# One masked minimum per score block, and the past's stages tied to their place, in a decoder-trunk kernel

## The chip, the cores and the metric

The kernel runs on one core of one Trainium2 chip. The metric is the device time of one execution in microseconds. The core has a matrix engine (TensorE, PE in the profile), a vector engine (VectorE, DVE), an activation engine (ScalarE, ACT), a general engine (GpSimd, POOL) and an engine that here only issues transfers (SyncE, SP). Each works through its own list of instructions in order, and semaphores tie the lists to one another.

## The reference

One inference step of one layer, for a prompt of 512 tokens and eight sample tokens that share the weights. All is fp32.

```python
m = ada_modulation(c)                           # shift, scale, gate, twice
h = rms_norm(x) * (1 + sc1) + sh1
xr, gr, q, k, v, fl, ga, gb = split(h @ w_in)   # D = 1024, 16 heads of 64
xc = causal_dwconv(xr, conv_buf, conv_w, conv_b)          # width 4
A = (rg_lru(xc) * gelu(gr)) @ w_proj_a
logf = log_sigmoid(fl + b_f);  F = cumsum(logf)
s = q.k / 8 + F[t] - F[s'],  masked to s' <= t            # prompt: blocks of 128 queries
B = (softmax(s) @ v) @ w_proj_b
x = x + g1 * ((sigmoid(ga) * A + sigmoid(gb) * B) @ w_o)
x = x + g2 * SwiGLU(rms_norm(x) * (1 + sc2) + sh2)        # then a last norm
```

The eight sample tokens attend to a paged cache of 1024 keys and values each (eight pages of 128 rows for each token), joined with their own new key and value. Their convolution takes the three inputs before from a state.

## The kernel before

Weights and activations are split into a high and a low part, and each product is three matmuls for each k-tile of 128 rows (high by high, low weight, low activation; L245, `half_product`). The 520 tokens are the free dimension, in two halves of 260. One product is a column tile of 128; its weights arrive by DMA (`wraw`), ACT makes the high part (`whi`, L210) and DVE the low one (`wlo`, L211), several products ahead.

A scheduler orders the instructions of each engine by a cost that it simulates while the program is built. An edge that adds no wait, `tc.issue_after(ins)`, keeps what follows behind `ins` on that instruction's engine; it can only shape the order.

Stages, in us of the profiled execution: norm, modulation and query products to 95; then eight rounds of convolution, recurrence and gates to 300; the first key product, branch A's projection and the first scores to 365; eight turns of prompt attention to 585, which this document numbers 1 to 8; branch B's projection and the merge to 640; the output projection to 700; and the FFN to the end.

A turn handles two heads. PE's list in turn n: the half `k_0` of the next key product; transposes of the value tile (`vt`); the half `k_1`; transposes of the probabilities (`ptt`); the half `v_0`; the second head's `ptt`; the next heads' first score blocks (`sc`); `v_1`; the values of the prompt (`po`); the other score blocks. ACT casts the keys (`ksA`, `ksB`, L985, the low parts by DVE at L988), the values (L1030) and the transposed probabilities (`ph`, L1086), takes the exponentials (L1067) and scales half of the probabilities (L1073). The last turn runs the last gate products instead of a key and a value product.

The decay rows of the two next heads (`decay_rows`) come in on SP as a broadcast of 512 numbers (`fb`, L1039); POOL adds the causal mask for the diagonal blocks (`fm`, L1041). In `scores`, DVE's custom operation adds decay and score and keeps the minimum over the row (scores carry a negative sign): once over the columns left of the diagonal block (L1064) and once over the diagonal block (L1065), which starts from the first minimum. Each is followed by a read of the accumulator. The minimum is the bias of the exponential.

The past runs beside all that in small steps, issued by `tick` (L644) at each product and four times a turn (`KEYS_AT`, `VALUES_AT`). Each key page of 512 KB is multiplied by the query and reduced on DVE (L629, L630). For two sample tokens at a time, a chain of five stages (`past_softmax`) then gives the weights of the past. Its last stage (`lgs`, L688) writes the sums out to memory through ACT (`mtd<-row`), and the last of the four chains has them loaded back (`mb<-mtd`). Value pages are multiplied on PE by calls of four matmuls (`pv`, L710), 32 calls in all; after each eighth, DVE picks the diagonal (`dr`, L716, L718), and a fold (`pvs`, L725, PE; copied by ACT) is issued at the next call. `join_weights` in the last turn joins past and present; its first DVE operation on loaded data is `mp`, L1138. In the convolution, three small DVE operations (L831) add the state's terms for the sample columns, in each of eight rounds.

Of the kernel before, what the change touches and what calls it, by code (L numbers as in the profile page):

```python
# [1 line left out]

# [6 lines left out]
F32 = mybir.dt.float32  # L9
F32R = mybir.dt.float32r  # L10
I32 = mybir.dt.int32
AF = mybir.ActivationFunctionType
ALU = mybir.AluOpType
AX = mybir.AxisListType
# [4 lines left out]
NP = 512  # L19
NS = 8  # L20
# [4 lines left out]
KT = 8  # L25
# [3 lines left out]
HALF = NT // 2  # L29
# [35 lines left out]
def kernel(ctx, tc, xT, par, gates, b_f, cst, cse, own, cache_k, cache_v, cache_lf, pt,  # L65
# [13 lines left out]
    def slot(name, cols=NT, dt=F32, parts=128):  # L79
        return heap.tile([parts, cols], dt, name=name, tag="slot")  # L80
# [4 lines left out]
    def small(name, parts, cols, bufs=4):  # L85
        return sm.tile([parts, cols], F32, name=name, tag="s_" + name, bufs=bufs)
# [151 lines left out]
    def half_product(n, j, a, out):  # L238
        hi, lo = splits[n]
        nk = units[n][2]  # L240
        t0, t1 = HALVES[j]
        for k in range(nk):
            ah, al = a(k, j) if callable(a) else (v[:, t0:t1] for v in a[k])
            for m, (wt, at) in enumerate(((hi, ah), (lo, ah), (hi, al))):
                pe.matmul(out[:, :HALF], lhsT=wt[k], rhs=at, start=k == 0 and m == 0, stop=k == nk - 1 and m == 2)  # L245

    def run_later(n):
        for fn in later.pop(n, []):
            fn()

    def product(name, a, evac, mid=None):
        n = begin()
# [390 lines left out]

    def tick(keys, values):  # L644
        key_sums()
        for c in list(chains):
            c[0] += 1
            if c[0] >= 2:
                c[0] = 0
                if next(c[1], True):  # L650
                    chains.remove(c)
        state["due"] += values
        state["due"] -= some_values(min(1, state["due"]))
        value_pages()
        key_pages(keys)

# [46 lines left out]
    def sample_values(r, j):  # L703
        if j == 0:
            pv[0] = bank(f"pv{r}")
        pgs = ahead.pop(0)
        for gq in range(4):
            c = 32 * j + 8 * gq
            hf = gq % 2
            pe.matmul(pv[0][32 * gq:32 * gq + 32, :], lhsT=pw[r][:, c:c + 32],  # L710
                      rhs=pgs[gq // 2][:, 512 * hf:512 * hf + 512], start=j == 0, stop=j == NPAGE - 1,
                      tile_position=(0, 32 * gq))
        if j == NPAGE - 1:
            pw[r] = None
            dr = slot("dr", 512)
            dve.tensor_tensor(dr, pv[0], pvm, ALU.mult)  # L716
            for n in (256, 128):
                dve.tensor_tensor(dr[:, :n], dr[:, :n], dr[:, n:2 * n], ALU.add)  # L718
            pv["todo"] = r, dr
        elif "todo" in pv:  # L720
            fold_values(*pv.pop("todo"))

    def fold_values(r, dr):
# [13 lines left out]
    def some_values(n):  # L737
        done = 0
        while done < n and values_todo and pw[values_todo[0][0]] is not None:
            value_pages()  # L740
            sample_values(*values_todo.pop(0))
            value_pages()
            done += 1
        return done
# [14 lines left out]
    def q_samples(b):  # L759
        t = slot("qt", 512, parts=NS)  # L760
        act.activation(t, qtp[b], AF.Copy, scale=DH ** -0.5)
        sp.dma_start(qtd[:, 512 * b:512 * b + 512], t)

    ready = []
    for i in range(KT):
        if i % 4 == 0:
            qtp.append(bank(f"qt{i}", NS))
        if i < 6:
            t = qpart[i]
            for j, (t0, t1) in enumerate(HALVES):  # L770
                b = bank(f"q{i}_{j}")
                for k in range(4):
                    q_matmuls(1, i, j, k, b)
                dve.tensor_tensor(t[:, t0:t1], b[:, :HALF], t[:, t0:t1], ALU.add)
        else:
            t = slot("q")
            product(f"q{i}", h, to(t, act.copy))
        if ready:
            q_done(*ready.pop())
        ready.append((i, t))  # L780
        if i == 3:
            split_upto(0)
        if i == 4:
            past_load()
            split_upto(1)
            close = forget_logits()
        if i == 6:
            close()
            with tc.issue_after(state["last"].ins), tc.issue_after(state["act"].ins):
                decay()  # L790
            past_turn(0)
        if i == 7:
            past_turn(1)
        if i >= 2:
            ada_piece(1, i - 2)
# [16 lines left out]
    def conv(i):  # L812
        gr = gate_load(i)
        if i + 1 < KT:
            gate_load(i + 1)
        xr, xc = slot("xr"), slot("xc")

        def evac(j, b):
            t0, t1 = HALVES[j]
            act.copy(xr[:, t0:t1], b)  # L820
            act.activation(xc[:, t0:t1], b, AF.Identity, scale=cw[3], bias=prm[:, i, P_CB:P_CB + 1])

        cw = [prm[:, i, P_CW + n:P_CW + n + 1] for n in range(4)]
        sc = prm[:, i, P_SC:P_SC + 24].rearrange("p (s n) -> p n s", n=3)
        co = conv_out[:, i, 3:27].rearrange("p (s n) -> p n s", n=3)
        product(f"xr{i}", h, evac)
        for n in range(3):
            d = 3 - n
            dve.scalar_tensor_tensor(xc[:, d:NP], xr[:, :NP - d], cw[n], xc[:, d:NP], ALU.mult, ALU.add)
        for n in range(3):  # L830
            dve.scalar_tensor_tensor(xc[:, NP:], sc[:, n], cw[n], xc[:, NP:], ALU.mult, ALU.add)  # L831
        pool.tensor_copy(conv_out[:, i, 0:3], xr[:, NP - 3:NP])
        pool.tensor_copy(co[:, 0:2], sc[:, 1:3])
        pool.tensor_copy(co[:, 2], xr[:, NP:])
        lru[i] = {"xc": xc}

        def close():
            gw = slot("gws", 512, F32R)
            act.copy(gw[:, :256], gr)
            dve.tensor_tensor(gw[:, 256:], gr, gw[:, :256].bitcast(F32), ALU.subtract)  # L840
            del gate_raw[i]
            lru[i].update(xs=split("xc", xc), gw=gw)

        defer(0, close)
# [188 lines left out]

    fbs, prob, pts = {}, {}, {}

    def decay_rows(i):
        for hd in (2 * i, 2 * i + 1):
            fb = slot("fb", 512)
            sp.dma_start(fb, ftd[hd:hd + 1, :].partition_broadcast(128))  # L1039
            fm = slot("fm", 512)  # L1040
            pool.tensor_tensor(fm.rearrange("p (b c) -> p b c", b=4), fb.rearrange("p (b c) -> p b c", b=4),  # L1041
                               msk.unsqueeze(1).to_broadcast([128, 4, 128]), ALU.add)
            fbs[hd] = fb, fm

    def scores(i, blocks):
        ks = kvs[i]["k"]
        qq, ql = kvs[i]["q"]
        mus = small("mu", 128, 16, 4).rearrange("p (c b a) -> p c b a", c=4, b=2)
        for b in blocks:
            n = 128 * b  # L1050
            for a, pr in enumerate(HEADS):
                hd = 2 * i + a
                fb, fm = fbs[hd]
                if b == 0:
                    prob[hd] = []
                    t3 = slot("p3", 512), slot("p02", 512), slot("p1", 256)
                    pts[hd] = (t3[1][:, :128], t3[2], t3[1][:, 128:], t3[0])
                sc = bank(f"sc{hd}_{b}")
                pe.matmul(sc[:, :n + 128], lhsT=qq[a][:, n:n + 128], rhs=ks[a][:, :n + 128], start=True, stop=False)
                pe.matmul(sc[:, :n + 128], lhsT=ql[a][:, n:n + 128], rhs=ks[a][:, :n + 128], start=False, stop=True)  # L1060
                p = pts[hd][b]
                mu = mus[:, :, b - blocks[0], a]
                if b:
                    dve.tensor_tensor_reduce(p[:, :n], fb[:, :n], sc[:, :n], 1.0, 3.0e38, ALU.add, ALU.min, mu[:, 0:1])  # L1064
                dve.tensor_tensor_reduce(p[:, n:n + 128], fm[:, n:n + 128], sc[:, n:n + 128], 1.0,  # L1065
                                         mu[:, 0:1] if b else 3.0e38, ALU.add, ALU.min, mu[:, 1:2])
                act.activation(p[:, :n + 128], p[:, :n + 128], AF.Exp, bias=mu[:, 1:2], scale=-1.0, accum_out=mu[:, 2:3])  # L1067
                prob[hd].append((p, mu))
        dve.reciprocal(mus[:, 3], mus[:, 2])
        for b in blocks:  # L1070
            for a in range(2):
                p, mu = prob[2 * i + a][b]
                (pool.tensor_scalar(p, p, mu[:, 3:4], None, ALU.mult) if a and i + 1 < KT else act.activation(p, p, AF.Copy, scale=mu[:, 3:4]))  # L1073

    def turn(i, a):
        hd = 2 * i + a
# [120 lines left out]
    for i in range(KT):  # L1197
        last = i + 1 == KT

        def mid_a():  # L1200
            v_tokens(i)
            if last:
                turn(i, 0)
            at(i, 0)
            if last:
                join_weights()

        def mid_b():
            if not last:
# [300 lines left out]
```

## Time and profile before

| | |
|---|---|
| median of three runs | 1085.54 us (1084.76 to 1086.71) |
| the profiled execution | 1088.77 us |
| its span, first to last instruction | 1087.0 us |
| mean granted TensorE clock | 0.981 |
| busy: PE, PEld, DVE, ACT, POOL | 96%, 88%, 62%, 46%, 14% |
| read from and written to HBM | 192.5 and 13.1 MB |

PE is matmul, PEld the load of weights beside it. An engine's row of 40 digits cuts the span into slices of 27.2 us, each digit the busy share in tenths. A wait is put down to the instruction whose end came last; "idle before" is time in which the engine had nothing that could start. In a row of matmuls the number before the colon of each form is partitions by columns. The turns start at about 367.8, 401.1, 426.9, 455.8, 482.2, 506.6, 543.2 and 565.8 us, where the first matmul of the key product (in the last turn, the gate) starts.

### The profile page before, as it was taken

The numbers are of one execution on the slowest core, as the hardware profiler recorded it, in microseconds if no ns is written. First come the engines' busy times: TensorE is split into PE (matmuls) and PEld (weight loads), VectorE is DVE, ScalarE is ACT, GpSimd is POOL, SyncE is SP. The second block draws the span as 40 slices with busy tenths as digits, with TensorE's granted clock in tenths as the row PEclk, the third lists the DMA queues.
The fourth block names the chain that finished last, engine by engine and source line by source line (L and its number), as shares of the span: only waits on it lengthen the run. The fifth ranks groups of instructions, "written<-read, shape, count | busy, mean of one in ns | idle before, by whom it ended". The sixth has DMA issues, their size and how long they took to land.

```text
span 1087.0 us, 20916 instructions
## 1 busy us (share of the span) xinstructions
PE 1038.3 (96%) x8210; PEld 954.5 (88%) x8210; DVE 674.6 (62%) x1261; ACT 495.1 (46%) x967; POOL 153.6 (14%) x201
## 2 busy tenths in 40 slices
PE   4999999999979989899799999999999999999996
PEld 2888999999969967687588989999999999999996
DVE  6434799979899988976375545943344333433355
ACT  4423576856831556677386224543212323222352
POOL 1102010100022514443130001500000000000013
PEclk9999999999989989999899999999999999999998
DMA  9796776689879998989843783222322422323212
GB/s 337 259 350 201 236 264 201 191 270 265 267 226 320 306 287 251 336 226 318 287 168 123 253 298 87 78 79 78 111 84 78 117 79 82 113 79 91 85 59 79
DMA packets 164996, 206.94 MB, mean 190 GB/s; under 512 B 9490, under 2 KB 125730, under 8 KB 164834
## 3 DMA queue, kind: packets, MB, share of 16 engines
q1 hardware_dynamic: 161170, 198.70, 58.5%
q10 hardware_dynamic: 3648, 6.39, 1.6%
q8 instruction: 64, 1.05, 0.4%
q0 software_dynamic: 80, 0.52, 0.2%
q14 instruction: 34, 0.28, 0.1%
HBM read 192.49 MB, written 13.09 MB: 189 GB/s over the span
## 4 chain that ended last, share of the span: by engine, by line
PE 76%; DVE 8%; DMA 6%; issue 4%; ACT 3%; POOL 1%; SPq 0%; POOLq 0%; DVEq 0%; ACTq 0%
PE fiu L245 11%; PE fig L245 11%; PE fo L245 8%; PE xr L245 4%; PE pb L245 4%; PE ga L245 4%; PE gr L245 3%; PE gb L245 3%; PE v L245 3%; PE k L245 3%; PE wo L245 3%; PE pa L245 2%; DMA pg<-in_cache_k_dram 2%; PE qp L450 2%; PE pv L710 2%
## 5 line engine op out<-in xcount | busy, mean ns | idle before, releaser
L211 DVE TENSOR_TENSOR wlo<-wraw,whi 128x1024 fp32r<-128x1024 f32 (+1 forms) x131 | 164.3, 1254 | 147.2 <-ACT whi L210 147.2
L210 ACT CAST whi<-wraw 128x1024 fp32r<-128x1024 f32 (+1 forms) x131 | 136.6, 1043 | 210.6 <-PE fo L245 74.7
L245 PE MATMUL fig<-h2h,whi 128*128 128x260 f32 x320 | 90.5, 283 | 0.0
L245 PE MATMUL fiu<-h2h,whi 128*128 128x260 f32 x320 | 90.5, 283 | 0.0
L245 PE MATMUL fiu<-h2h,wlo 128*128 128x260 f32 x320 | 90.5, 283 | 0.0
L245 PE MATMUL fig<-h2h,wlo 128*128 128x260 f32 x320 | 90.5, 283 | 0.0
L245 PE MATMUL fiu<-h2l,whi 128*128 128x260 f32 x320 | 90.2, 282 | 0.0
L245 PE MATMUL fig<-h2l,whi 128*128 128x260 f32 x320 | 90.2, 282 | 0.0
L245 PE MATMUL fo<-ach,wlo 128*128 128x260 f32 x292 | 82.7, 283 | 0.0
L245 PE MATMUL fo<-acl,whi 128*128 128x260 f32 x292 | 82.7, 283 | 0.0
L245 PE MATMUL fo<-ach,whi 128*128 128x260 f32 x292 | 82.5, 282 | 0.0
L630 DVE TENSOR_REDUCE S<-pg 128x16 f32<-128x1024 f32 x64 | 76.6, 1211 | 1.3 <-POOL pg L617 1.0
L629 DVE TENSOR_TENSOR pg<-pg,qb 128x1024 f32<-128x1024 f32 x60 | 74.8, 1260 | 3.0 <-DMA pg<-in_cache_k_dram 3.0
L320 POOL TENSOR_TENSOR ss<-ss,sq 128x260 f32<-128x260 f32 x18 | 13.6, 755 | 422.7 <-ACT sq L319 422.3
L245 PEld LDWEIGHTS fiu<-h2l,whi 128*128 128x128 f32 x320 | 60.3, 189 | 0.0
L245 PEld LDWEIGHTS fig<-h2l,whi 128*128 128x128 f32 x320 | 60.3, 189 | 0.0
L245 PEld LDWEIGHTS fig<-h2h,wlo 128*128 128x128 f32 x320 | 60.3, 188 | 0.0
L245 PEld LDWEIGHTS fiu<-h2h,wlo 128*128 128x128 f32 x320 | 60.3, 188 | 0.0
L245 PEld LDWEIGHTS fig<-h2h,whi 128*128 128x128 f32 x320 | 60.3, 188 | 0.0
L245 PEld LDWEIGHTS fiu<-h2h,whi 128*128 128x128 f32 x320 | 60.3, 188 | 0.0
L245 PEld LDWEIGHTS fo<-ach,whi 128*128 128x128 f32 x292 | 55.1, 189 | 0.0
L245 PEld LDWEIGHTS fo<-ach,wlo 128*128 128x128 f32 x292 | 55.0, 188 | 0.0
(378 smaller groups left out, 3380.2 us busy)
## 6 DMA issues: line engine op xcount, KB each, us to landing
pg<-in_cache_k_dram SPq DMA_DIRECT2D x64, 512.0 KB, 5.7
pg<-in_cache_v_dram SPq DMA_DIRECT2D x64, 512.0 KB, 6.2
araw<-in_ada_w_dram SPq DMA_DIRECT2D x48, 512.0 KB, 7.3
wraw<-in_w_fi_dram SPq DMA_DIRECT2D x44, 512.0 KB, 5.2
wraw<-in_w_in_dram SPq DMA_DIRECT2D x34, 512.0 KB, 8.2
wraw<-in_w_in_dram SPq DMA_DIRECT2D x11, 1024.0 KB, 6.3
wraw<-in_w_fo_dram SPq DMA_DIRECT2D x8, 1024.0 KB, 5.2
x<-in_xT_dram SPq DMA_DIRECT2D x16, 260.0 KB, 5.8
```

The lines of the kernel that those rows point to most:

```text
L210: state["act"] = act.copy(hi[:, :k1 - k0], src)
L211: state["last"] = dve.tensor_tensor(lo[:, :k1 - k0], src, hi[:, :k1 - k0].bitcast(F32), ALU.subtract)
L245: pe.matmul(out[:, :HALF], lhsT=wt[k], rhs=at, start=k == 0 and m == 0, stop=k == nk - 1 and m == 2)
L320: eng.tensor_tensor(acc[:, t0:t1], acc[:, t0:t1], q_, ALU.add)
L450: pe.matmul(b[:, :HALF], lhsT=wt, rhs=at[:, t0:t1], start=k == 0 and m == 0, stop=k == 3 and m == 2)
L629: dve.tensor_tensor(pg, pg, q, ALU.mult)
L630: dve.tensor_reduce(S[r // 2][:, c:c + H], pg.rearrange("p (h d) -> p h d", d=DH), AX.X, ALU.add)
L710: pe.matmul(pv[0][32 * gq:32 * gq + 32, :], lhsT=pw[r][:, c:c + 32], rhs=pgs[gq // 2][:, 512 * hf:512 * hf + 512], start=j == 0, stop=j == ...
```

## The change

Four edits.

The minimum of a block is taken by one DVE operation over all its columns. So decay and mask stand side by side in the block's own order: ACT copies the first 256 columns of `fb` into `fm`, POOL adds the mask to four pieces of 128 columns (one of them in `fb`, one into a new small tile `f0`). Block 0 reads `f0`, block 1 two pieces of `fm`, block 2 the first 384 columns of `fm`, and block 3 `fb`. A row of `mu` falls away.

The steps of the chains and of the past's values in `tick`, and `join_weights` in the last turn, are held behind the last product matmul on PE, the last weight split on DVE and the last on ACT that the program had written by then (`in_place`). Key pages are not.

The fold of a finished group is issued at the third call of the next group, not at its first.

The state's terms of the convolution are computed once for all eight rounds (`past_conv`, eight products and one sum in the query stage), and each round adds them with one DVE operation.

```diff
@@ half_product
             for m, (wt, at) in enumerate(((hi, ah), (lo, ah), (hi, al))):
-                pe.matmul(out[:, :HALF], lhsT=wt[k], rhs=at, start=k == 0 and m == 0, stop=k == nk - 1 and m == 2)
+                state["mm"] = pe.matmul(out[:, :HALF], lhsT=wt[k], rhs=at, start=k == 0 and m == 0,
+                                        stop=k == nk - 1 and m == 2)
...
+    @contextmanager
+    def in_place():
+
+        with tc.issue_after(state["mm"].ins), tc.issue_after(state["last"].ins), tc.issue_after(state["act"].ins):
+            yield
@@ tick
         key_sums()
-        for c in list(chains):
...
-        state["due"] += values
-        state["due"] -= some_values(min(1, state["due"]))
+        with in_place():
+            for c in list(chains):
...
+            state["due"] += values
+            state["due"] -= some_values(min(1, state["due"]))
         value_pages()
         key_pages(keys)
@@ sample_values
-        elif "todo" in pv:
+        elif j == 2 and "todo" in pv:
             fold_values(*pv.pop("todo"))
@@ the query stage
+    conv_past = keep.tile([128, KT, NS], F32, name="conv_past")
+
+    def past_conv():
+        t = slot("cvp", KT * 24).rearrange("p (k s n) -> p k s n", k=KT, s=NS)
+        for i in range(KT):
+            dve.tensor_tensor(t[:, i], prm[:, i, P_SC:P_SC + 24].rearrange("p (s n) -> p s n", n=3),
+                              prm[:, i, P_CW:P_CW + 3].unsqueeze(1).to_broadcast([128, NS, 3]), ALU.mult)
+        dve.tensor_reduce(conv_past, t, AX.X, ALU.add)
...
                 decay()
+                past_conv()
             past_turn(0)
@@ conv
-        for n in range(3):
-            dve.scalar_tensor_tensor(xc[:, NP:], sc[:, n], cw[n], xc[:, NP:], ALU.mult, ALU.add)
+        dve.tensor_tensor(xc[:, NP:], xc[:, NP:], conv_past[:, i], ALU.add)
@@ decay_rows
         for hd in (2 * i, 2 * i + 1):
+            a = hd % 2
+            if a == 0:
+                f0 = slot("f0", 256)
             fb = slot("fb", 512)
             sp.dma_start(fb, ftd[hd:hd + 1, :].partition_broadcast(128))
             fm = slot("fm", 512)
-            pool.tensor_tensor(fm.rearrange("p (b c) -> p b c", b=4), fb.rearrange("p (b c) -> p b c", b=4),
-                               msk.unsqueeze(1).to_broadcast([128, 4, 128]), ALU.add)
-            fbs[hd] = fb, fm
+            act.copy(fm[:, :256], fb[:, :256])
+            for dst, b in ((f0[:, 128 * a:128 * a + 128], 0), (fm[:, 384:], 1), (fm[:, 256:384], 2), (fb[:, 384:], 3)):
+                pool.tensor_tensor(dst, fb[:, 128 * b:128 * b + 128], msk, ALU.add)
+            fmb = fm.rearrange("p (b c) -> p b c", b=4)
+            fbs[hd] = f0[:, 128 * a:128 * a + 128], fmb[:, 0::3], fm[:, :384], fb
@@ scores
-                if b:
-                    dve.tensor_tensor_reduce(p[:, :n], fb[:, :n], sc[:, :n], 1.0, 3.0e38, ALU.add, ALU.min, mu[:, 0:1])
-                dve.tensor_tensor_reduce(p[:, n:n + 128], fm[:, n:n + 128], sc[:, n:n + 128], 1.0,
-                                         mu[:, 0:1] if b else 3.0e38, ALU.add, ALU.min, mu[:, 1:2])
...
+                ins = p[:, :n + 128], sc[:, :n + 128]
+                if b == 1:
+                    ins = [t.rearrange("p (b c) -> p b c", b=2) for t in ins]
+                dve.tensor_tensor_reduce(ins[0], fbs[hd][b], ins[1], 1.0, 3.0e38, ALU.add, ALU.min, mu[:, 0:1])
...
@@ the last turn
             if last:
-                join_weights()
+                with in_place():
+                    join_weights()
```

Three places show how the order moves. The first is PE's list in turn 6, from the last transposes of the first probabilities to the value product; a row of `pv` with x4 is one call. Before:

```order
L1082 MATMUL ptt_1_7310<-cs,p_7025 128x128
L1082 MATMUL ptt_1_7310<-cs,p_7024 128x128 x2
L688 MATMUL lgs_7319<-mk,cs 128x32
L710 MATMUL pv_7324<-pg,pw 32x512 x20
L725 MATMUL pvs_7329<-cs,dr 128x16
L245 MATMUL v_0_7366<-hh,whi 128x260
```

And now:

```order
L1105 MATMUL ptt_1_7332<-cs,p_7044 128x128
L1105 MATMUL ptt_1_7332<-cs,p_7043 128x128 x2
L696 MATMUL lgs_7341<-mk,cs 128x32
L718 MATMUL pv_7346<-pg,pw 32x512 x4
L245 MATMUL v_0_7385<-hh,whi 128x260
L245 MATMUL v_0_7385<-hh,wlo 128x260
```

Of the five calls that stood there one is left, and the fold is gone from this place. By the calls in PE's list, turns 1 to 8 held 3, 3, 3, 4, 3, 5, 2.25 and 0.75 calls, in 4, 5, 3, 6, 4, 5, 3 and 1 groups of up to four matmuls; now they hold 3, 3, 3, 3, 3, 3, 4 and 2, in 3, 3, 3, 4, 3, 3, 5 and 2. Most turns now have one call behind `vt`, one behind the first `ptt` and one at the turn's end. Eight calls stand ahead of turn 1, as before.

The second is DVE's list in turn 6, where the first operation of `join_weights` on the loaded sums stood between a weight split and the key splits. Before:

```order
L1008 SCALAR_TENSOR_TENSOR qlB<-qB,qqB 128x512
L211 TENSOR_TENSOR wlo<-wraw,whi 128x1024
L1138 TENSOR_TENSOR mp<-mb,lf 16x8
L988 TENSOR_TENSOR ksA<-k_0_7198,ksA 64x260
L988 TENSOR_TENSOR ksB<-k_0_7198,ksB 64x260
L1031 TENSOR_TENSOR v_7233<-vt_7228,v_7233 128x2x128
```

Now it stands a turn later, among the minima (ISA rows) of the last scores at the end of turn 7:

```order
L1089 ISA p_7827,mu<-fm,sc_1_7838 128x256
L1089 ISA mu 128x1
L1092 RECIPROCAL mu<-mu 128x4
L211 TENSOR_TENSOR wlo<-wraw,whi 128x1024
L1161 TENSOR_TENSOR mp<-mb,lf 16x8
L1089 ISA p_7818,mu<-fm,sc_2_7931 128x384
```

The third is ACT's list in turn 5, from the weight split to the key and value casts. Before:

```order
L210 CAST whi<-wraw 128x1024
L985 CAST ksA<-k_0_6810 64x260
L985 CAST ksB<-k_0_6810 64x260
L986 COPY kt<-k_0_6810 128x260
L1030 CAST v_6845<-vt_6840 128x2x2x64
```

And now:

```order
L210 CAST whi<-wraw 128x1024
L1063 COPY fm<-fb 128x256 x2
L1002 CAST ksA<-k_0_6829 64x260
L1002 CAST ksB<-k_0_6829 64x260
L1003 COPY kt<-k_0_6829 128x260
L1047 CAST v_6864<-vt_6859 128x2x2x64
```

The two copies of the decay rows, which wait for the rows to land, stand between the split and the casts. On SP a load of a value page (`pg<-in_cache_v`) stands ahead of the second row in turns 5, 6 and 7, and it waits until the `pv` call behind `vt` of the same turn has freed a page's place.

More of the change, by code (lines that the diff above doesn't have):

```diff
@@ L1 @@
-from contextlib import ExitStack, nullcontext
+from contextlib import ExitStack, contextmanager, nullcontext
 import numpy as np
@@ L645, in tick @@
         key_sums()
-        for c in list(chains):
[L647 to L651, printed above, removed]
-        state["due"] += values
-        state["due"] -= some_values(min(1, state["due"]))
+        with in_place():
+            for c in list(chains):
+                c[0] += 1
+                if c[0] >= 2:
+                    c[0] = 0
+                    if next(c[1], True):
+                        chains.remove(c)
+            state["due"] += values
+            state["due"] -= some_values(min(1, state["due"]))
         value_pages()
@@ L1047, in scores @@
         qq, ql = kvs[i]["q"]
-        mus = small("mu", 128, 16, 4).rearrange("p (c b a) -> p c b a", c=4, b=2)
+        mus = small("mu", 128, 12, 4).rearrange("p (c b a) -> p c b a", c=3, b=2)
         for b in blocks:
@@ L1052, in scores @@
                 hd = 2 * i + a
-                fb, fm = fbs[hd]
                 if b == 0:
@@ L1062, in scores @@
                 mu = mus[:, :, b - blocks[0], a]
-                if b:
-                    dve.tensor_tensor_reduce(p[:, :n], fb[:, :n], sc[:, :n], 1.0, 3.0e38, ALU.add, ALU.min, mu[:, 0:1])
-                dve.tensor_tensor_reduce(p[:, n:n + 128], fm[:, n:n + 128], sc[:, n:n + 128], 1.0,
-                                         mu[:, 0:1] if b else 3.0e38, ALU.add, ALU.min, mu[:, 1:2])
-                act.activation(p[:, :n + 128], p[:, :n + 128], AF.Exp, bias=mu[:, 1:2], scale=-1.0, accum_out=mu[:, 2:3])
+                ins = p[:, :n + 128], sc[:, :n + 128]
+                if b == 1:
+                    ins = [t.rearrange("p (b c) -> p b c", b=2) for t in ins]
+                dve.tensor_tensor_reduce(ins[0], fbs[hd][b], ins[1], 1.0, 3.0e38, ALU.add, ALU.min, mu[:, 0:1])
+                act.activation(p[:, :n + 128], p[:, :n + 128], AF.Exp, bias=mu[:, 0:1], scale=-1.0, accum_out=mu[:, 1:2])
                 prob[hd].append((p, mu))
-        dve.reciprocal(mus[:, 3], mus[:, 2])
+        dve.reciprocal(mus[:, 2], mus[:, 1])
         for b in blocks:
@@ L1072, in scores @@
                 p, mu = prob[2 * i + a][b]
-                (pool.tensor_scalar(p, p, mu[:, 3:4], None, ALU.mult) if a and i + 1 < KT else act.activation(p, p, AF.Copy, scale=mu[:, 3:4]))
+                (pool.tensor_scalar(p, p, mu[:, 2:3], None, ALU.mult) if a and i + 1 < KT else act.activation(p, p, AF.Copy, scale=mu[:, 2:3]))
     def turn(i, a):
```

## The prediction

> **What bounds the kernel now.** I read the page first: the first line is the busy time of each engine, the next three cut the span into 40 slices of 27.2 us (tenths).
>
> ```profile
> PE 1038.3 (96%) x8210; PEld 954.5 (88%) x8210; DVE 674.6 (62%) x1261; ACT 495.1 (46%) x967; POOL 153.6 (14%) x201
> PE   4999999999979989899799999999999999999996
> PEclk9999999999989989999899999999999999999998
> DMA  9796776689879998989843783222322422323212
> ```
>
> TensorE is the bound. Work taken from another engine is worth nothing unless PE stands still for it, so the question is where PE has holes that the change touches. Slices with a 7 stand at 11 and 19. The table of stretches shows the convolution's stage (95 to 300 us) and then, about turn by turn, the eight prompt-attention turns (us; PE, PEld, DVE, ACT, POOL busy; granted clock, DMA share, GB/s).
>
> ```profile
> 95.00:300.00 205.00, 205.00 (x1671) 193.78 (x1664) 178.87 (x255) 137.67 (x242) 13.04 (x24) 1.00 0.76 238
> 365.00:400.00 35.00, 30.68 (x202) 24.33 (x201) 30.88 (x60) 17.97 (x46) 13.91 (x12) 0.90 0.99 286
> 400.00:427.00 27.00, 26.74 (x185) 21.13 (x185) 25.01 (x59) 18.89 (x46) 12.23 (x9) 1.00 0.87 252
> 427.00:456.00 29.00, 25.57 (x181) 20.11 (x180) 25.45 (x62) 16.91 (x42) 11.94 (x9) 1.00 0.99 335
> 456.00:482.00 26.00, 26.00 (x184) 19.77 (x184) 20.77 (x52) 18.97 (x47) 9.71 (x9) 1.00 0.96 293
> 482.00:507.00 25.00, 25.00 (x185) 20.49 (x183) 17.48 (x56) 18.77 (x46) 9.36 (x10) 1.00 0.87 246
> 507.00:543.00 36.00, 29.32 (x194) 22.20 (x193) 15.75 (x48) 17.66 (x44) 8.42 (x9) 0.86 0.95 298
> 543.00:566.00 23.00, 23.00 (x174) 19.68 (x173) 16.34 (x52) 18.45 (x46) 7.82 (x7) 1.00 0.59 199
> ```
>
> In turns 1 to 3 DVE is busy almost throughout (30.9 of 35, 25.0 of 27, 25.5 of 29) and the DMA share is 0.87 to 0.99; turns 4, 5 and 7 are full PE; turn 6 is the odd one: 36 us where its neighbours take 23 to 26, DVE only 15.8 busy, clock 0.86. The chain of waits over turn 6 (start, us, what) tells why.
>
> ```profile
> 512.94 1.05 ACT whi L210
> ...
> 514.17 4.32 DMA mtd<-row
> ...
> 518.55 5.34 DMA mb<-mtd
> ...
> 523.91 0.32 DVE mp L1138
> ...
> 529.34 4.67 PE v L245 x24
> ...
> 536.25 2.88 PE v L245 x24
> ```
>
> The merge's first operation mp stands in DVE's queue directly behind a weight split. It needs sums that go out to memory (4.32 us) and come back (5.34 us); behind it stand the key splits, the value split and the fold's operations. Here are the wait in DVE's timeline, the bunched value matmuls in PE's, and PE's own waits for value pages (total us, times, longest).
>
> ```profile
> 523.91 0.32 DVE L1138 TENSOR_TENSOR mp<-mb,lf 16x8 f32<-16x8 f32 x1 [8.66 <-DMA mb<-mtd]
> 522.17 1.39 PE L710 MATMUL pv<-pg,pw 128*32 128x512 f32 x4 [4.69 <-DMA pg<-in_cache_v_dram]
> PE pv L710 <- DMA pg<-in_cache_v_dram: 6.2, 2, 4.7
> ```
>
> PE thus stops twice in one place: for value pages, because five calls of the past's values run together, and then for DVE.
>
> **Chains, merge and folds in place.** The merge's operations go behind the last turn's splits, a turn after the sums were written: at least 23 us for a round trip of 9.7. The sums' store on ACT and their load on SP stay in turn 6; nothing is late on their account. The five calls together become one, the others go to turn boundaries. Turn 6: the split of 512.94 ends with PE's k; ptt, lgs and one value call then take some 2 us, so v starts at about 514.9 instead of 529.3: 14.5 us, and 1.8 more because the cold v of 4.67 becomes 2.88. Two value calls come in elsewhere in the turn, minus 2.0: 14.3 gained. By the table, 36 minus a turn like turn 5 with one call less (24) is 12. I take 13.
>
> What a call costs, and a piece of one (8 records are a whole call, 2 a quarter of it):
>
> ```profile
> 464.25 1.06 PE L710 MATMUL pv<-pg,pw 128*32 128x512 f32 x8
> 468.79 1.05 PE L710 MATMUL pv<-pg,pw 128*32 128x512 f32 x2
> ```
>
> A quarter costs as much as the whole, about 1.0 us: what counts is the number of groups. By the order, turns 1 to 8 go from 4, 5, 3, 6, 4, 5, 3, 1 groups to 3, 3, 3, 4, 3, 3, 5, 2. Turn 6 is in the 13 already. In PE-bound turns that is -2 (4), -1 (5), +2 (7), +1 (8), and one split call more in the gates' stage: +1.0 us together. In turns 1 and 2 PE waits for others anyway: 0.
>
> **One minimum per block.** The rows of DVE, 365 to 590 us (busy us, mean ns):
>
> ```profile
> L1065 DVE CUSTOM_DVE_ANT_0 p<-fm,sc,mu 128x128 f32<-128x128 f32 x45 | 14.3, 342 | 0.2
> L1064 DVE CUSTOM_DVE_ANT_0 p<-fb,sc 128x384 f32<-128x384 f32 x16 | 8.5, 547 | 0.1
> L1064 DVE CUSTOM_DVE_ANT_0 p<-fb,sc 128x256 f32<-128x256 f32 x14 | 5.4, 415 | 1.0 <-PE sc L1060 1.0
> L1065 DVE DVE_READ_ACCUMULATOR2_ANT mu<- 128x1 f32 x59 | 4.8, 81 | 0.0
> L1064 DVE CUSTOM_DVE_ANT_0 p<-fb,sc 128x128 f32<-128x128 f32 x14 | 3.5, 282 | 1.1 <-PE sc L1060 1.1
> ```
>
> Each 128 columns more cost 0.13 us (282, 415, 547), so 512 are estimated at 680. Block 1: 282+81+342+81 becomes 415+81; block 2: 415+81+342+81 becomes 547+81; block 3: 547+81+342+81 becomes 680+81: 0.29 us each, 0.87 a head, 1.74 a turn. PE-bound turns get nothing of it. In turns 1 to 3, DVE-bound, the ceiling is 3 x 1.74 = 5.2 and the floor 0, where key pages set the pace (DMA share to 0.99). I take half, 2.6.
>
> The price is paid on POOL and ACT: four adds of 128 columns a head instead of one of 512, and a copy of 256 columns on ACT. Nearest rows (POOL's 128x8 and 128x512 adds; min/median/max of the latter; ACT's copy of 260 columns):
>
> ```profile
> L993 POOL TENSOR_TENSOR qk<-kt,q 128x8 f32<-128x8 f32 x8 | 3.5, 443 | 44.5 <-ACT kt L986 44.5
> L1041 POOL TENSOR_TENSOR fm<-fb,cs x16: 1262/1277/3922, 314.6 to 553.0; 128x512 f32<-128x512 f32 x16
> L986 ACT COPY kt<-k x14: 375/375/379, 377.4 to 552.6; 128x260 f32<-128x260 f32 x14
> ```
>
> An add of 128 columns lies between 0.44 and 1.28, by interpolation 0.64: 2.6 a head for 1.28. POOL is busy 8 to 14 us of a turn, so 2.6 more a turn is covered. ACT has 16 copies, 6 us, some 0.75 a turn beside 18 busy: covered as busy time. Not covered is the wait. Only POOL waited for the row fb to land so far; now ACT does, and directly behind the copies stand the key casts ksA, ksB, the value casts and ph. Turn 5 of before shows both times, with the landing of all such loads:
>
> ```profile
> 489.69 0.36 ACT L985 CAST ksA<-k 64x260 fp32r<-64x260 f32 x1
> 493.79 1.30 POOL L1041 TENSOR_TENSOR fm<-fb,cs 128x512 f32<-128x512 f32 x1 [4.08 <-DMA fb<-ftd]
> DMA to landing us min/median/max: 3.4/6.2/7.8
> ```
>
> The row came 4.1 us after ACT wanted to cast. In the new order the second head's row also stands on SP behind a value page that waits for the value call after vt, half a turn's k later than the first. Bounds for a turn: 0 (the row is there, as in turn 7 of before) to 4.1 plus 7.8-6.2, 5.7. I take 4, 3.5 and 2 in turns 5, 6 and 7, less 1 us that PE has in hand each (the value call between ptt and v): 6.5. Turns 1 to 3 hide it behind DVE, turn 4's first copy stands ahead with the split.
>
> **Convolution.** Its row, with a 128x8 DVE operation for the new add:
>
> ```profile
> L831 DVE SCALAR_TENSOR_TENSOR xc<-prm,xc x24: 208/220/224, 103.3 to 263.0; 128x8 f32<-128x8 f32 x24
> L883 DVE TENSOR_TENSOR gate<-gate,th x8: 131/140/150, 159.4 to 300.4; 128x8 f32<-128x8 f32 x8
> ```
>
> 24 x 0.22 = 5.3 becomes 8 x 0.14 = 1.1 plus nine small operations in the query stage, about 2 us at the same price: 2 us less of DVE. That stage has PE at 205.00 of 205 us: 0. Were DVE late there, it would be worth 2 at most.
>
> **Sum.** -13 + 1.0 - 2.6 + 6.5 = -8.1 us. Against the profiled execution (1088.77) that is 1080.7. It lies 3.2 above the median of 1085.54; from the median, 1077.4. About 0.2%, 2.2 us, is what a measurement can tell from no change.
>
> **Rivals.**
> ACT waits in every turn (slower). The copies stand ahead of the key casts in turns 1 to 7. If each of turns 2 to 7 waits 5.7 us less 1 in hand, that is 28 us against 14.6 of gain without any: 1099; at 4.1, 19 against 14.6: 1090. It decides above 2.4 us per turn. For it: DMA share 0.87 to 0.99 and page loads ahead of each row on SP. Against: in turns 1 to 3 PE is waiting for DVE meanwhile. Likely value 1090.
>
> Value pages wait at their new places. The 6.2 us of PE's page waits come back in full: -1.9, 1083.6, at the edge of no change. Against: three calls a turn need six pages, 3 MB in 24 us, beside the 246 to 298 GB/s (6 to 7 MB) that such turns move.
>
> POOL's adds come late for the minimum. Before, one add took up to 3922 ns where most take 1277, so something held POOL for 2.6 us. PE's first score of turn 5 (its minimum follows) stands 16 us into the turn that began at 482:
>
> ```profile
> 498.48 0.31 PE L1059 MATMUL sc<-ksA,qqA 128*128 128x128 f32 x1
> ```
>
> The second head's row came 12 us into it. Were each of the four adds held for 1.3, half of that excess, a head would take 4 x 1.94 = 7.8 us and the minimum would be some 3 us late; in turns 5 and 6 that is +6: 1083.4. The Trainium skill, page SBUF — State Buffer, section Who interferes with whom, says that a DVE instruction with two SBUF inputs contends with a GpSimd instruction that reads SBUF, and that the loser waits for the whole instruction. By that rule more and smaller adds are more chances to be held; the row's maximum agrees, its median says that it is rare.
>
> ACT never waits and DVE's gain comes in full: -13 + 1 - 5.2 = -17.2, 1068.3. For it: turn 7's row was early.
>
> **Chances.** Forecast 0.50; ACT in every turn 0.18; pages 0.10; POOL 0.08; the full gain 0.14. Pages and POOL lie at the bound, half of each on either side. Faster 0.50 + 0.14 + 0.09 = 0.73, same 0.09, slower 0.18. The range goes from the full gain, 1067, to 1088, which leaves out most of the slower case.
>
> **What would show it.** mp without a wait for mb, at the end of turn 7; no group of 20 value rows; turn 6 near 25 us at clock 1.0; minima of 0.28, 0.41, 0.55 and 0.68 us, one read each; in ACT's waits, fm for fb, 2 to 4 us in turns 5 to 7, and ksA or ph late for ptt behind it. Wrong would be: turn 6 still above 30, ACT's waits for fb above 15 us in sum, or PE waiting for value pages at the turn boundaries.

## The result

The changed kernel takes 1084.9 us (median of 20 runs, 1082.1 to 1089.9), the kernel before 1085.47 in as many runs beside it: a ratio of 1.0001, 95% interval 0.9989 to 1.0013. Nothing that can be measured was gained where 8.1 us were forecast. The time lies inside the stated range of 1067 to 1088, but 7.5 us above the 1077.4 that was forecast from the median; "same" had been given 9 in 100.

The two profiled executions differ by more than the medians: 1088.77 before, 1084.21 after. The one of before is 3.3 us above its median, the other 0.7 below. So a second profile of each was taken, and what follows uses both.

The profile after, with the lines that answer to those shown of before. First busy time and the 40 slices (27.1 us each).

```profile
PE 1035.1 (96%) x8210; PEld 955.1 (88%) x8210; DVE 663.6 (61%) x1158; ACT 498.9 (46%) x983; POOL 161.3 (15%) x249
PE   4999999999979989998999999999999999999996
PEclk9999999999999989998999999999999999999998
DMA  9795776679779988898875773223323422323212
```

DVE has 11 us less to do, ACT 4 and POOL 8 more. The hole of slice 19 is gone and a shallower one has come in slice 18. The table of the turns, cut at the changed kernel's own turn starts:

```profile
369.00:402.00 33.00, 28.10 (x183) 22.93 (x183) 28.25 (x49) 15.29 (x40) 14.07 (x17) 0.84 0.90 288
402.00:430.00 28.00, 25.41 (x178) 20.89 (x177) 22.73 (x42) 17.95 (x45) 12.09 (x16) 0.94 0.85 237
...
481.00:511.00 30.00, 26.50 (x182) 22.57 (x178) 16.19 (x40) 18.31 (x47) 9.14 (x16) 0.89 0.91 267
511.00:537.00 26.00, 24.58 (x187) 20.02 (x180) 16.70 (x41) 18.95 (x49) 9.90 (x15) 1.00 0.81 224
```

Turn 6 is short now (26 us, clock 1.00), as forecast. Turn 5 is the long one, 30 us at a clock of 0.89. The lengths of all stretches, from the first matmul of one to the first of the next (us; "start" is what lies before turn 1, "pb" is branch B's projection and the merge; the numbers in brackets are those of the experiments below):

| | start | 1 | 2 | 3 | 4 | 5 | 6 | 7 | 8 | pb |
|---|---|---|---|---|---|---|---|---|---|---|
| before | 367.8 | 33.3 | 25.8 | 28.9 | 26.4 | 24.3 | 36.6 | 22.7 | 19.4 | 54.7 |
| before, again | 367.7 | 31.9 | 25.8 | 30.3 | 26.4 | 24.3 | 34.6 | 22.7 | 19.4 | 54.7 |
| changed | 368.8 | 32.9 | 28.3 | 26.4 | 24.6 | 30.4 | 25.4 | 25.3 | 20.0 | 52.7 |
| changed, again | 367.3 | 35.8 | 29.9 | 25.2 | 24.4 | 30.4 | 27.4 | 26.2 | 20.0 | 52.7 |
| copies on POOL (3) | 368.1 | 35.5 | 29.8 | 25.1 | 25.0 | 23.6 | 24.5 | 25.4 | 20.0 | 52.8 |
| and ties from turn 3 (5) | 368.7 | 35.0 | 26.5 | 25.3 | 25.0 | 23.7 | 24.9 | 25.4 | 20.0 | 52.8 |

The chain of waits through turn 5 of the changed kernel:

```profile
486.65 8.32 DMA fb<-ftd
494.99 0.40 ACT fm L1063
495.39 0.27 ACT ksA L1002
495.68 0.37 ACT ksB L1002
496.06 0.39 ACT kt L1003
496.47 0.42 DVE ksA L1005
496.90 0.43 DVE ksB L1005
...
498.82 1.09 PE ptt L1105 x4
...
501.69 4.64 PE v L245 x24
```

The decay row of the second head is issued at 486.65, 5.6 us into the turn, and takes 8.32 us to land, where the view of before has 3.4 to 7.8 for its 14 loads in the turns. ACT stands at its copy, the key casts come behind it, DVE's low parts behind those, and PE's transposes wait for the bank they share. The product v behind it runs cold: 4.64 us where 2.88 is normal. ACT's waits in turns 5 and 6, and PE's in turn 5:

```profile
ACT fm L1063 <- DMA fb<-ftd: 8.3, 4, 4.1
PE ptt L1105 <- DVE ksB L1005: 3.5, 2, 2.8
```

The operations themselves cost what was forecast, to a few ns, or less: DVE's minima (mean ns behind the bar) and POOL's four adds (min/median/max ns).

```profile
L1089 DVE CUSTOM_DVE_ANT_0 p<-fb,sc 128x512 f32<-128x512 f32 x14 | 9.3, 682 | 0.2
L1089 DVE CUSTOM_DVE_ANT_0 p<-fm,sc 128x384 f32<-128x384 f32 x14 | 7.3, 544 | 0.9 <-PE sc L1083 0.9
L1065 POOL TENSOR_TENSOR fm<-fb,cs x32: 450/461/2980, 315.4 to 547.7; 128x128 f32<-128x128 f32 x32
L1161 DVE TENSOR_TENSOR mp<-mb,lf 16x8 f32<-16x8 f32 x1 | 0.1, 146 | 0.0
```

682 ns for 512 columns, 415 for the two pieces of block 1, as for 256 columns in one piece before; 0.46 for an add of 128; and mp waits for nothing.

### The profile page after: what moved, and what is told of

Its sections match the earlier page's. It is cut to its first block, busy times and chain, and to the rows that moved or that the text cites. A ratio compares the mean times of both kernels' runs of the same rounds, so it can differ in the third digit from the quotient of the medians.

```text
span 1082.1 us, 20877 instructions
## 1 busy us (share of the span) xinstructions
PE 1035.1 (96%) x8210; PEld 955.1 (88%) x8210; DVE 663.6 (61%) x1158; ACT 498.9 (46%) x983; POOL 161.3 (15%) x249
## 4 chain that ended last, share of the span: by engine, by line
PE 81%; DVE 7%; DMA 5%; ACT 2%; issue 2%; POOL 1%; SPq 1%; POOLq 0%; DVEq 0%
PE fiu L245 11%; PE fig L245 11%; PE fo L245 10%; PE gb L245 4%; PE xr L245 4%; PE pb L245 4%; PE ga L245 4%; PE v L245 4%; PE pa L245 3%; PE gr L245 3%; PE wo L245 3%; DMA fb<-ftd 2%; PE k L245 2%; PE pv L718 2%; PE qp L457 2%
## 5 line engine op out<-in xcount | busy, mean ns | idle before, releaser
L245 PE MATMUL fiu<-h2h,whi 128*128 128x260 f32 x320 | 90.9, 284 | 0.0
L327 POOL TENSOR_TENSOR ss<-ss,sq 128x260 f32<-128x260 f32 x18 | 13.6, 757 | 420.3 <-ACT sq L326 419.8
L636 DVE TENSOR_TENSOR pg<-pg,qb 128x1024 f32<-128x1024 f32 x60 | 72.4, 1224 | 0.2 <-DMA pg<-in_cache_k_dram 0.2
L245 PEld LDWEIGHTS fo<-acl,whi 128*128 128x128 f32 x292 | 55.0, 188 | 0.0
```

Of the source, the lines that this page charges most:

```text
L245: state["mm"] = pe.matmul(out[:, :HALF], lhsT=wt[k], rhs=at, start=k == 0 and m == 0, stop=k == nk - 1 and m == 2)
L327: eng.tensor_tensor(acc[:, t0:t1], acc[:, t0:t1], q_, ALU.add)
L636: dve.tensor_tensor(pg, pg, q, ALU.mult)
```

## The experiments

Three theories were to be told apart. A: ACT's wait for the decay rows gives back what the ties gain. B: the first profile of before was long in turn 6 by chance and there is little to gain. C, formed after the first four: in the DVE-bound turns 1 and 2 the ties take away value calls that had filled PE's waits.

Experiments 1 to 4, 5 to 8 and 9 to 12 each ran beside a set of runs of before, with medians of 1083.57, 1087.19 and 1087.30. Since these differ by up to 3.7 us, kernels of different sets are compared by their ratios to before; where medians are given across sets, they carry that difference.

**1. The ties alone**

The changed kernel with `scores`, `decay_rows` and the convolution as before; what remains is:

```diff
+        with in_place():
             for c in list(chains):
...
-        elif "todo" in pv:
+        elif j == 2 and "todo" in pv:
...
+                with in_place():
+                    join_weights()
```

> The kernel before with the in-place ties and the later fold alone: two minima a block, no copy of decay rows on ACT, convolution as before. Theory A (the copy's wait on ACT gives back what the ties gain): turn 6 short as in the changed kernel, turn 5 near 24 instead of 30 us, 5 to 8 us below the kernel before. Theory B (the profiled execution of before was long by chance and turn 6 has little to give): within 2 us of the kernel before.

1082.39 us, ratio 0.9982 (0.9964 to 0.9999). Turns 4 to 8 do what A says: 24.1, 23.6, 24.6, 25.4, 20.8, together 118.5 where before has 129.4 and 127.4. But turns 1 to 3 rise from 88.0 to 92.0. By the profiles the ties alone gain 9 to 11 us in one place and give back 4 in another, a loss that was in no theory and stands in turn 2 (29.8 for 25.8). The runs show less than that difference, 1.2 us by medians and 2.0 by ratio: A's number is missed, and the whole alone would fit B's. What takes the rest is not shown; the 27 runs of before in this set lie between 1079.74 and 1087.80.

**2. The one minimum alone**

The kernel before with the new `decay_rows` and `scores`, copies on ACT.

```diff
+            act.copy(fm[:, :256], fb[:, :256])
...
+                dve.tensor_tensor_reduce(ins[0], fbs[hd][b], ins[1], 1.0, 3.0e38, ALU.add, ALU.min, mu[:, 0:1])
```

> The kernel before with the one minimum alone, with its copies on ACT and its four adds on POOL; the five value calls and the merge's first operation stay in turn 6. Theory A: the copy's wait on ACT costs PE 3 to 6 us in turns 3 to 5, so 3 to 6 us above the kernel before. Theory B: within 2 us of it.

1091.62 us, ratio 1.0066 (1.0041 to 1.0091): slower by 7 to 8 us, a little more than A's 3 to 6. Turn 5 is 29.4 (24.3 before) and turn 6 is 38.7; ACT waits 13.7 us for the rows, up to 6.9 at a time:

```profile
ACT fm L1046 <- DMA fb<-ftd: 13.7, 4, 6.9
```

**3. The changed kernel with its copies on POOL**

```diff
-            act.copy(fm[:, :256], fb[:, :256])
+            pool.tensor_copy(fm[:, :256], fb[:, :256])
```

> The changed kernel with the copy of 256 columns on POOL instead of ACT. Theory A: ACT waits for no decay row, turn 5 falls from 30 to about 25 us, 4 to 6 us below the changed kernel. Theory B, or POOL as the next to be late: within 2 us of the changed kernel.

1077.8 us, ratio 0.9939 (0.9919 to 0.9960): some 6 to 7 us below the changed kernel by ratio as by medians. Turn 5 falls from 30.4 to 23.6, turn 6 to 24.5. The place is shown by one line of edit: the engine that waits for the row. POOL, which now copies and adds, is not late for the minimum: in the turns DVE waits for none of its adds or copies.

Experiment 1 ran in the same set and differs from this kernel by the one minimum and the convolution. Its median of 1082.39 lies 4.6 us above this one's, and the two intervals of the ratio do not meet. So with the ties in every turn the one minimum, its copies on POOL, is worth some 4 us (the convolution alone gives nothing, experiment 12); the turn lengths show 1.7 of that in turns 1 to 3, where turn 3 falls from 28.1 to 25.1 and turn 1 grows by 1.3.

**4. The merge's operations alone in place**

```diff
-                join_weights()
+                with in_place():
+                    join_weights()
```

> The kernel before with the merge's operations alone in place; the five value calls stay together in turn 6. If DVE's wait for the sums is what makes turn 6 long, 5 to 9 us below the kernel before; if PE's wait for value pages takes its place, 1 to 3 us; theory B: within 2 us.

1083.02 us, ratio 0.9988 (0.9969 to 1.0007): not to be told from before. Turn 6 is 35.0. DVE no longer waits for the sums, but PE's chain leads through the same store:

```profile
513.63 4.19 DMA mtd<-row
517.82 0.02 issue
517.84 0.02 SPq L171
...
518.82 5.49 DMA pg<-in_cache_v_dram
524.31 0.04 issue
524.36 3.22 PE pv L717 x8
```

The load of the sums waits on SP (L171) for the store; the value page for the bunched calls stands behind it on SP and takes 5.49 us to land from there. So the two waits of turn 6 lie over each other, behind one store.

**5. Ties from turn 3 on, copies on POOL**

```diff
+        state["place"] = i >= 2
...
-        with in_place():
+        with in_place() if state["place"] else nullcontext():
```

> The third experiment's kernel (changed, copies on POOL), with the past's steps tied from turn 3 on, so that in turns 1 and 2 a value call again stands ahead of lgm and lgs. Theory C (in the DVE-bound turns the calls that stood there filled PE's wait for DVE, and the ties took them away): turns 1 and 2 fall from 65.3 to 59 to 61 us, the whole 3 to 6 us below the third experiment's. Rival (DVE and the pages alone set the length of these turns): turns 1 and 2 stay within 2 us of 65, and so does the whole.

1076.19 us, ratio 0.9884 (0.9862 to 0.9906): the fastest of all, 1.2% below before. Turns 1 and 2 fall from 65.3 to 61.5 us, near the forecast, 3.3 of it in turn 2; the whole is 0.6% below the third experiment's by ratio, 1.6 us by medians and 2.6 by the spans of the profiles (1077.5 and 1074.9), so the size of it is between 2 and 6 us. PE's waits in turns 1 and 2 (366 to 434 us; `lgm` and `lgs` are products of the chains on PE, `pl` is the low part of the transposed probabilities), first of experiment 3:

```profile
PE lgm L685 <- DVE pl L1110: 3.8, 1, 3.8
PE ptt L1105 <- DVE ksB L1005: 2.7, 1, 2.7
PE lgs L696 <- DVE pl L1110: 2.1, 1, 2.1
```

and of this one:

```profile
PE lgm L685 <- DVE pl L1110: 2.9, 1, 2.9
PE ptt L1105 <- DVE ksB L1005: 2.7, 1, 2.7
PE lgs L696 <- DVE pl L1110: 1.4, 1, 1.4
```

With a value call ahead of lgm and lgs each wait is 0.7 to 0.9 shorter, and the call itself, 1.0 us, no longer stands at the turn's end. In turn 2 the clock does the rest. The chain through the product behind lgs, and the stretch with its clock (the number before the DMA share), first of experiment 3:

```profile
422.81 5.49 PE v L245 x24
404.00:433.00 29.00, 25.92 (x177) 22.04 (x176) 22.61 (x40) 17.10 (x42) 12.57 (x18) 0.88 0.90 263
```

and of this one:

```profile
423.05 3.14 PE v L245 x24
404.00:430.00 26.00, 24.30 (x178) 19.75 (x177) 23.42 (x44) 17.50 (x46) 13.93 (x17) 1.00 0.94 300
```

The same 24 matmuls take 2.35 us less.

**6. The one minimum alone, copies on POOL**

Experiment 2 with experiment 3's line.

> The kernel before with the one minimum alone, its copies on POOL: the second experiment without ACT's wait. Theory A: 5 to 8 us below the second experiment, within 3 us of the kernel before. Rival (the copy and the four adds themselves are too slow): within 2 us of the second experiment.

1088.07 us, ratio 1.0002 (0.9984 to 1.0020). Against 1.0066 with copies on ACT: the wait was worth 0.6% here too. And the one minimum, freed of it, gains nothing that can be measured in this order. That is a sum of two things: turn 3 is 25.5 where the two profiles of before have 28.9 and 30.3, but turns 5 and 6 are 26.8 and 39.3 where they have 24.3 and 34.6 to 36.6, and PE waits up to 6.6 us for a value page.

**7 and 8. Both kernels once more**

> The kernel before once more, for a second profile. If its first one was long in turn 6 by chance (theory B), turn 6 is 31 us or less; if the ties' place in turn 6 is always long, 35 to 38 us, and what made the first profile long lies elsewhere.

> The changed kernel once more. If ACT's wait for the decay rows is of its order and not chance, turn 5 is 28 to 31 us again and ACT waits 12 to 18 us for the rows in sum; if it was chance, turn 5 is about 25.

Turn 6 of before is 34.6, turn 5 of the changed kernel 30.4 again, and ACT waits 13.1 us for the rows. The 34.6 is just under the 35 to 38 that was expected of a place that is always long, and far from 31. Theory B falls: both long turns belong to the order. What differs from run to run is in turns 1 to 3 of the changed kernel (87.6 and 90.9) and in turn 6 of either by 2.

**9. Rows ahead of the value pages on SP**

The changed kernel, copies on ACT; each page load is placed behind the rows that the program had issued by then.

```diff
+        row = tc.issue_after(state["row"].ins) if "row" in state else nullcontext()
+        with row, tc.issue_after(loads[-4].ins) if len(loads) >= 4 else nullcontext():
...
+            state["row"] = sp.dma_start(fb, ftd[hd:hd + 1, :].partition_broadcast(128))
```

> The changed kernel, copies on ACT, but with the two rows of a turn ahead of that turn's value pages on SP; value calls are split into halves more often, some five groups more. Theory A (the copy waits because the second row stands behind a page that waits for PE): ACT's waits for the rows fall below 4 us in sum, turns 5 and 6 to 24 to 27 us, 2 to 6 us below the changed kernel. Rival (the copy itself and ACT's order are what is slow): turn 5 stays near 30 and the whole within 2 us of the changed kernel.

1083.68 us, ratio 0.9966 (0.9952 to 0.9980), 0.35% below the changed kernel's. Turns 5 and 6 are 24.8 both, as A says. ACT still waits 3.0 us once in turn 5 and 6.4 in turn 1, 9.4 in sum where less than 4 was expected; but the copies of turn 5 start 7.4 and 8.7 us into the turn instead of 9.5 and 14.0, early enough that PE waits for nothing behind them. Turn 1 becomes 39.6: there PE waits 6.4 us for a value page that now stands behind the rows. The queue's order is a cause in turn 5 beside the engine, and to turn it around moves the wait to turn 1.

**10. Ties from turn 3 on, alone**

Experiment 5 with two minima and the convolution of before.

> The kernel before with the ties from turn 3 on and the later fold alone: two minima, convolution as before. If the one minimum, once its copies wait on no matmul's engine, gives DVE's time in the DVE-bound turns: 2 to 5 us above the fifth experiment's, 6 to 9 us below the kernel before. If it gives nothing (as the sixth says): within 1.5 us of the fifth experiment's, some 11 us below the kernel before.

1076.55 us, ratio 0.9900 (0.9881 to 0.9918). Within 0.4 us of experiment 5 by medians and 1.7 by ratio, with intervals that overlap: with the ties placed so, minimum and convolution give nothing that can be told. The gain is the ties'. Against experiment 1, which has the ties in every turn, it is 0.8% lower by ratio, and turns 1 to 3 fall from 92.0 to 88.4, as experiment 5 has it.

**11. As the first, the merge's operations untied**

```diff
-                with in_place():
-                    join_weights()
+                join_weights()
```

> The first experiment's kernel with the merge's operations not tied: the five value calls are apart, but mp stands in turn 6, now behind the split of the first transposes. If the two waits of turn 6 lie over each other (each hides the other), turn 6 is 29 to 34 us, against 24.6 with both gone and 35.0 with the calls together: 4 to 8 us above the first experiment's. Rival (the bunched calls alone make turn 6 long): turn 6 below 26.

1087.41 us, ratio 1.0004 (0.9991 to 1.0017), against the first experiment's 0.9982: 0.2% or 2.4 us by ratio, less than the 4 to 8 expected (the medians lie 5.0 apart, but so do those of before by 3.7). Turn 6 is 29.8, inside the 29 to 34: the calls are apart and mp still makes DVE wait, and PE behind it for `pl`.

```profile
DVE mp L1146 <- DMA mb<-mtd: 2.7, 1, 2.7
PE v L245 <- DVE pl L1095: 2.8, 1, 2.8
```

With experiment 4 it closes the square for turn 6: both there 34.6 to 36.6 (the two profiles of before), the calls alone 35.0, mp alone (a little later in DVE's list) 29.8, neither 24.6. To undo one of the two parts alone brings 0 to 7 us of the 11.

**12. The convolution alone**

```diff
-        for n in range(3):
-            dve.scalar_tensor_tensor(xc[:, NP:], sc[:, n], cw[n], xc[:, NP:], ALU.mult, ALU.add)
+        dve.tensor_tensor(xc[:, NP:], xc[:, NP:], conv_past[:, i], ALU.add)
```

> The kernel before with the convolution's sample terms at once alone. All theories: PE has no hole between 140 and 280 us, so within 2 us of the kernel before; if DVE were late there, up to 2 us below.

1086.39 us, ratio 0.9994 (0.9976 to 1.0013). PE had no hole there and nothing came of it. Its operations cost 0.158 us for each add and 0.176 for each product, near the forecast.

## Why the prediction was wrong, point by point

**Turn 6** was right in mechanism and place: mp waits for nothing, no group of 20 value rows is left, and by the mean of the two pairs of profiles the turn falls from 35.6 to 26.4, 9.2 us, where 13 less 2.5 of ACT's wait had been taken.

**The groups of value calls** were right: turn 4 by -1.8 and -2.0 for -2, turn 8 +0.6 for +1, turn 7 +2.6 and +3.5 for +2 and 1 of ACT. In turn 7 it was the calls alone: experiments 1 and 3, in which ACT waits for no row, have the same 25.4.

**ACT's wait for the rows** is one of the two terms that failed. The hazard was named, with its engine and its queue, but turn 5 was taken at 4 us less 1 in hand. It measured +6.1 us in both profiles, and without the wait (experiment 3) the turn is 6.8 shorter. The 4 came from the wrong row: the 4.1 that the prediction read is the lateness of the first head's row, and ACT has to copy both before its casts. POOL's add of the second row, in the two profiles of before:

```profile
495.79 1.27 POOL L1041 TENSOR_TENSOR fm<-fb,cs 128x512 f32<-128x512 f32 x1 [0.70 <-PE pv L710]
496.01 1.27 POOL L1041 TENSOR_TENSOR fm<-fb,cs 128x512 f32<-128x512 f32 x1 [0.73 <-DMA fb<-ftd]
```

That is 6.1 us behind the cast of 489.69 in the first of them (the wait is put down to PE there, to the row in the second). In the changed kernel the second row is there 14.0 us into the turn, hardly later than these 13.6, and ksA starts at 495.30, 5.5 us behind the end of the split. The second part that was left out is the clock. In that turn, with 3.5 us of waits on PE, it is 0.89, and the product behind takes 1.8 us more; the same cold v stood in turn 6 of before, where it was counted as a gain, and was not charged to the new wait. There was no microsecond in hand either: the keys' low parts, behind which PE's transposes wait (`ptt <- DVE ksB`), come after the casts. As a whole the term came out near the 6.5 that were forecast, 6.7 by the ratios of experiment 3 and the changed kernel, but that is in part luck: by the profiles turn 5 had 6.8 for 3, turn 6 1.9 for 2.5 and turn 7 0.4 for 1.

**Turns 1 and 2** are the other one. They were costed at nothing for the groups, "PE waits for others anyway". That step failed: a call ahead of an operation that waits is free because PE waits, and one that is moved to the turn's end is not; and the longer wait left a lower clock to the product behind it. Experiment 5 shows it, by 3.8 us in the two turns, and experiment 10 against 1 by 3.6 in the first three. In the runs it is more, 6 and 9 us by ratio; what makes it more is not shown. The runs make this the larger failure of the two: for the ties -13 + 1.0 = -12 us had been taken, and they give 2.0 us with turns 1 and 2 tied (experiment 1) and 10.9 without (experiment 10).

**The minimum in DVE-bound turns** was taken at half of 5.2. Turns 1 to 3 went from 88.0 in both profiles to 87.6 and 90.9, the loss of the ties included. By the runs experiments 6 and 10 give the minimum nothing, and 1 against 3 gives it some 4 us; by the lengths of turns 1 to 3 it is 1.7 (1 against 3), 1.6 (10 against 5) and 0.1 (6). So a gain is there in some orders and not in others; which page or place decides it is not shown. Its durations were right to 4 ns.

**Convolution**: 0, as said.

The two pairs add up: by the means of the profiles, turns 1 to 3 +1.3, turn 4 -1.9, turn 5 +6.1, turn 6 -9.2, turn 7 +3.1, turn 8 +0.6, the start +0.3, pb -2.0, together -1.7, beside -0.6 of the medians. Against the sum of the prediction that is 4.1 in turn 5, 3.9 in turns 1 to 3 (by experiment 5 nearly all of it the ties) and 1.3 in turn 6, less 2.0 in pb and 0.9 in small parts. What pb gave had been in no term: it is 54.7 at a clock of 0.97 in both profiles of before and 52.7 at 1.00 in those after. It does not go with the change: the same stage is 53.2 and 53.1 at 1.00 in experiments 4 and 12, and 54.5 and 54.8 at 0.97 in 2 and 11.

Of the rivals, ACT's wait in every turn did not come true in the first profile of the changed kernel: turn 4 shows none and turns 2 and 3 waits of 1.2 and 3.3 us. Pages did not wait at their new places. POOL's adds were held up to 2.98 us for a median of 0.46, so the row that spoke for that rival comes back. The longest, at 321.04 us, ran beside DVE's page product and weight split of 1.20 and 1.21 us, each with two inputs from SBUF, as the rule cited from the Trainium skill (page SBUF — State Buffer, section Who interferes with whom) would have it. But no minimum waited for it in the profiles of the kernels with one minimum, and POOL could take the copies too.

## What to carry to other kernels

An engine that has to wait for a transfer must have nothing urgent behind that instruction; give such an instruction to the engine with the emptiest list (here POOL, whose copy of 256 columns took 0.40 us, as ACT's did). When a wait for several transfers is costed, take the last of them. When a stall is costed, add the cold clock of what runs after it, on the new stall as on the old. And work that stands out of its place may be filling somebody's wait: tie it where PE is full, and leave it where PE waits.

## What was not expected of the hardware

A broadcast row of 512 numbers, issued 0.4 us behind a 512 KB page, took 8.32 us to land with the DMA share at 0.91; that the page is the reason is not shown. And a wait that stands in one queue may hide another behind the same store: freeing DVE of the sums' round trip (4.3 and 5.3 us) left turn 6 at 35.0 us, because SP, waiting for the same store, held a value page back for as long.
